# Starting the split weights of each stage 16 bytes further into longer tiles, in a one-core decoder block

## The chip, the cores and the metric

The kernel runs on one core of one Trainium2 chip. The metric is the device time in microseconds, as the median of three runs of the same kernel. Its work goes over five engines that run side by side: TensorE (PE, with its weight loads shown apart as PEld), VectorE (DVE), ScalarE (ACT), GpSimd (POOL) and SyncE (SP), which issues most transfers.

## What is computed

The reference is one layer of a decoder block on x of 512 tokens by 2048 features, all in float32. It is, cut to what matters:

```python
def reference(x, ...):
    h = rmsnorm(x, attn_pre_norm)
    m = token_mixer(h, w_in, ...)          # proj = h @ w_in (6160 columns)
                                           # 4 heads of gated linear attention, 4 of differential attention
                                           # concatenated, then @ w_o (2048 x 2048)
    x = x + rmsnorm(m, attn_post_norm)
    h = rmsnorm(x, ffn_pre_norm)
    f = conv_ffn(h, w_ffn_in, conv_w, conv_b, w_ffn_out)
    return x + rmsnorm(f, ffn_post_norm)

def conv_ffn(h, w_ffn_in, conv_w, conv_b, w_ffn_out):
    up = h @ w_ffn_in                      # 2048 x 11264
    a, b = up[..., :D_FF], up[..., D_FF:]  # D_FF = 5632
    a = causal depthwise convolution of a, width 3
    return (gelu(a) * b) @ w_ffn_out       # 5632 x 2048
```

## The kernel before

**Products in three parts.** TensorE multiplies in a reduced float32 format, so every operand is held as a high and a low part: `hi` is the value rounded to that format and `lo` the remainder. A product is the sum of three matmuls, hi·hi, hi·lo and lo·hi, into one bank of PSUM. The activations stand for a whole stage in the tiles `ah` and `al`. The weights come from HBM in granules of 128 partitions by 1024 values: `load` brings one into a tile `raw` (four buffers), and `granule` (L106) makes its two parts, `whi` on ACT (L114) and `wlo` on DVE (L115). Both have three buffers of 4096 bytes in each partition, so the split can run at most two granules ahead of the matmuls that read it. All of these buffers, and each slice of them that a matmul reads, begin at a multiple of 256 bytes within the partition. Where `granule` is given a `spare` pool, the parts go to the tiles `xhi` and `xlo` instead.

**Two kinds of matmul.** In `mm_t` (L150 to L152) and in the products of the first feed-forward matrix, `up_prods` (L897 to L899), the weights are the stationary operand, 128 by 128, and the activations stream past, 512 or 256 columns of them. In `mm_n` (L168 to L170), `down_prods` (L994 to L996) and the last part (L1101 to L1103) the activations are stationary and 512 columns of the weights stream.

**Stages in order of time.** `first_half` norms and transposes x and starts the first projection. The mixer follows: `proj_n` and `proj_t` compute the projections of w_in, and between their granules the function `step` lets small pieces of the attention heads run (the list `fill`). Then comes the output projection (three columns by `proj_n`, the fourth written out by hand in `to_ffn`), which ends in the first matmuls of the feed-forward part. The rest of that part uses a seven-product scheme for 2x2 blocks: 20 units `ups` of the first matrix, two for each of ten groups, then 10 units `downs` of the second. A unit has seven segments (x0, z0, y0, z1, x1, y1, y2) of two granules. After every second up unit, `token_sums` writes the products of this group to DRAM: three of the blocks as they are and four sums, s5, s2, s7 and s3 in this order, each added on DVE into a tile of 256 KB with the tag `sum` (L965) and put out by a transfer on SP. The down units read them back.

**What sets the order.** In three places the order on PE, ACT, DVE and POOL is the program's own (`manual_schedule`). Elsewhere a scheduler orders the instructions ahead of time, from its own estimate of when each can start; on the chip each engine then works through its list in order. When a pool of tiles is closed and another takes its place (`fa.close()`, then the pool `ff`), the first writers of the new pool wait until all work on the old one is done, its transfers to DRAM among them.

**Other pools that the change touches.** `small` holds columns of statistics (eight buffers of each), the tag `tmp` of the pool `mx` holds the working tiles of the attention heads (six buffers), and the tag `sum` those of `token_sums` (four buffers).

Of the kernel before, what the change touches and what calls it, by code (L numbers as in the profile page):

```python
# [9 lines left out]
F32 = mybir.dt.float32  # L10
F32R = mybir.dt.float32r
# [6 lines left out]
P = 128  # L18
D = 2048
S = 512  # L20
# [3 lines left out]
GH, GDK, GDV, RANK = 4, 128, 256, 16  # L24
# [6 lines left out]
GR = 1024  # L31
# [4 lines left out]
def hybrid_layer(ctx: ExitStack, tc: tile.TileContext, x, attn_pre_norm, w_in, w_alpha_up, b_alpha,  # L36
# [10 lines left out]
    def dma(o, i):  # L47
        return nc.sync.dma_start(out=o, in_=i)
# [7 lines left out]
    mm = nc.tensor.matmul  # L56

    const = ctx.enter_context(tc.tile_pool(name="const", bufs=1))
    small = ctx.enter_context(tc.tile_pool(name="small", bufs=8, side="right"))
    few = ctx.enter_context(tc.tile_pool(name="few", bufs=1, side="right"))  # L60
    psm = ctx.enter_context(tc.tile_pool(name="psm", bufs=4, space=PSUM))
    psa = ctx.enter_context(tc.tile_pool(name="psa", bufs=4, space=PSUM))
# [12 lines left out]
    wpool = ctx.enter_context(tc.tile_pool(name="w", bufs=3))  # L75

    def bank(pool=None):
        return (pool or psa).tile([P, 512], F32, name="bank", tag="bank")
# [5 lines left out]
    def step(n=None):  # L84
        pace[1] += pace[0]
        while pace[1] >= 1.0:
            pace[1] -= 1.0
            while fill:
                try:
                    next(fill[0])  # L90
                    break
                except StopIteration:
                    fill.pop(0)
# [6 lines left out]
    def load(src, a):  # L100
        raw = wpool.tile([P, GR], F32, name="raw", tag="raw", bufs=4)
        dma(raw.rearrange("p (a b) -> p a b", a=a), src)
        return raw

    def granule(src, a, raw=None, spare=None, bufs=4):
        if raw is None:  # L106
            raw = load(src, a)
        if spare:
            hi = spare.tile([P, GR], F32R, name="xhi", tag="xhi", bufs=bufs)
            lo = spare.tile([P, GR], F32R, name="xlo", tag="xlo", bufs=bufs)  # L110
        else:
            hi = wpool.tile([P, GR], F32R, name="whi", tag="whi")
            lo = wpool.tile([P, GR], F32R, name="wlo", tag="wlo")
        act(hi, raw, AF.Copy)  # L114
        tt(lo, raw, hi.bitcast(F32), ALU.subtract)  # L115
        r = "p (a b) -> p a b"
        return hi.rearrange(r, a=a), lo.rearrange(r, a=a)
# [24 lines left out]
    def mm_t(banks, g, w, t0, t1):  # L142
        for n in range(2):
            for k in range(4):
# [6 lines left out]
                mm(o, wh, al[:, t0:t1, kk, :], start=False, stop=False)  # L151
                mm(o, wl, ah[:, t0:t1, kk, :], start=False, stop=sp)  # L152


    def proj_t(w3, col, emit):
        banks = [bank(psm) for _ in range(2)]
        for g in range(KT // 4):
            mm_t(banks, g, granule(w3[:, 4 * g:4 * g + 4, col:col + 256], 4), 0, NT)
            if g == KT // 4 - 1:
                for n in range(2):  # L160
                    emit(n, banks[n])
            step()
# [8 lines left out]


    def proj_n(w3, col, emit, order=tuple(range(KT)), first=0, banks=None):
        if banks is None:
            banks = [bank(psm) for _ in range(NT)]
        for g in range(first, KT // 2):
            w = granule(w3[:, order[2 * g]:order[2 * g] + 2, col:col + 512], 2)
            for t in range(NT):
                mm_n(banks, t, g, w)
                if g == KT // 2 - 1:  # L180
                    emit(t, banks[t])
            step()
# [3 lines left out]
    mx = mixer.enter_context(tc.tile_pool(name="mx", bufs=6))  # L186

    def big8(name):
        return mx.tile([P, 2048], F32, name=name, tag="big8", bufs=6)
# [2 lines left out]
        return mx.tile([P, S], F32, name=name, tag="qk", bufs=6)  # L192

    def tmp(name, shape=(P, S)):
        return mx.tile(list(shape), F32, name=name, tag="tmp")


    def first_half(c):
# [150 lines left out]

    def forget_gate():  # L350
        gar = tmp("gar").rearrange("p (k r) -> p k r", r=RANK)[:, :KT, :]
        dma(gar, w_in3[:, :, C_GA:C_GA + RANK])
        gas = mx.tile([P, KT, 80], F32R, name="gas", tag="big8", bufs=6)
        nc.vector.memset(gas.bitcast(F32), 0.0)
        split(gas[:, :, 0:RANK], gas[:, :, 64:64 + RANK], gar)
        wup = mx.tile([80, GH * GDK], F32, name="wup", tag="tmp")
        nc.vector.memset(wup, 0.0)
        dma(wup[0:RANK, :], w_alpha_up[0])
        dma(wup[64:64 + RANK, :], w_alpha_up[0])
        yield  # L360
        gab = bank()
        gav = gab[:80, :].rearrange("p (t c) -> p t c", c=P)
        for k in range(KT):
            mm(gav, gas[:, k, :], ah[:, :, k, :], start=k == 0, stop=False)
            mm(gav, gas[:, k, :], al[:, :, k, :], start=False, stop=k == KT - 1)
        gaT = mx.tile([80, S], F32, name="gaT", tag="tmp")
        nc.vector.tensor_copy(gaT, gab[:80, :])
        yield

        a = big8("za")  # L370
        for h in range(GH):
            zb = bank()
            mm(zb, wup[:, h * P:(h + 1) * P], gaT, start=True, stop=True)
            bcol = cols[:, h:h + 1]
            act(a[:, h * S:(h + 1) * S], zb, AF.Abs, bias=bcol)
            ts(bcum[h], zb, bcol, 0.0, ALU.add, ALU.min)
            if h % 2:
                yield
# [241 lines left out]
    def to_ffn():  # L620
# [91 lines left out]
        mm_t(bb2, 3, wb[3], 2, 4)  # L712
        return ba, list(zip(bb, bb2))

    with tc.manual_schedule(engines=IN_ORDER):
        ba, bb = to_ffn()
    wo.close()
# [13 lines left out]
    fp = fa.enter_context(tc.tile_pool(name="fa", bufs=2))  # L731
# [223 lines left out]
    def token_sums(gi, u0, u1):  # L955
        c, i = (gi - 1) // 2, (gi - 1) % 2
        T = [slice(0, 256), slice(256, 512)]
        a11, a21, a12, a22 = u0[:, :, T[0]], u0[:, :, T[1]], u1[:, :, T[0]], u1[:, :, T[1]]

        def put(n, src):  # L960
            dma(sd[c][n][:, i, :].rearrange("p (n t) -> p n t", n=2), src)

        def add(n, x, y, op):
            t = fp.tile([P, 2, 256], F32, name=n, tag="sum", bufs=4)
            tt(t, x, y, op)  # L965
            put(n, t)
            return t

        put("a11", a11)
        put("a12", a12)  # L970
        put("a22", a22)
        s5 = add("s5", a21, a22, ALU.subtract)
        s2 = add("s2", s5, a11, ALU.subtract)
        add("s7", a11, a21, ALU.subtract)
        add("s3", s2, a12, ALU.add)
# [50 lines left out]
    for i, u in enumerate(ups):  # L1026
        nxt = ups[i + 1] if i + 1 < len(ups) else None
        if i == 0:
            u.x0()
            u.z0()  # L1030
        u.y0()
        u.z1()
        if i == 0:
            for h, r in enumerate(s7raw):
                split(up["s7"][0][:, h], up["s7"][1][:, h], r)
        if nxt is None:
            prepare(0, "a11", flat_tile())
        u.x1()
        if nxt is None:
            prepare(0, "s5", flat_tile())  # L1040
        u.y1()
        if nxt is not None:
            nxt.x0()
            u.y2()
            nxt.z0()
        else:
            downs = [down_unit(c, cb) for c in range(NG // 2) for cb in range(2)]
            prepare(0, "s2", flat_tile())
            downs[0].x0()
            prepare(0, "s3", flat_tile())  # L1050
            u.y2()
# [8 lines left out]
    for i, u in enumerate(downs):  # L1060
        nxt = downs[i + 1] if i + 1 < len(downs) else None
        nc_ = (i + 1) // 2
        first = i % 2 == 0
        last_cb = i % 2 == 1 and nxt is not None

        if first and i:
            prepare(i // 2, "s3")
        u.y0()
        if first:
            prepare(i // 2, "a12")  # L1070
        u.z1()
        if first:
            prepare(i // 2, "s7")
        u.x1()
        if first:
            prepare(i // 2, "a22")
        if last_cb:
            prepare(nc_, "a11")
        u.y1()
        if last_cb:  # L1080
            prepare(nc_, "s5")
        if nxt is not None:
            nxt.x0()
        if last_cb:
            prepare(nc_, "s2")
        u.y2()
        if nxt is not None:
            nxt.z0()


    def ffn_out_weights(gi, c):
# [65 lines left out]
    for q, at in enumerate(((3, 1), (0, 0))):  # L1157
        raw = ff.tile([P, GR], F32, name="st", tag="st", bufs=4)
        dma(raw, ud0[:, 2 * q:2 * q + 2, :].rearrange("p n t -> p (n t)"))
        hi, lo = (piece(v, *at) for v in (ah, al))  # L1160
# [34 lines left out]
```

## Time and profile before

| | |
|---|---|
| three runs | 2189.55, 2192.62 and 2193.9 us, median 2192.62 |
| the profiled execution's own time | 2189.8 us |
| its span, first to last instruction | 2188.1 us |
| PE busy | 2152.7 us (98%), 13009 matmuls |
| DVE busy | 1418.9 us (65%) |
| ACT busy | 901.2 us (41%) |
| POOL busy | 204.6 us (9%) |
| mean granted TensorE clock | 0.996 |

All times of an event are counted from the first instruction. Busy time of PE counts overlapping matmuls once, so a PE at 100% only says that there was always a matmul under way. The pace of the matmuls is better read from how many of them fall into a window of time. In the tables of groups each row has a line of the kernel, an engine, an operation, the tiles written and read, the count, the busy time and the mean duration in ns of one, and then the time that the engine stood idle just before it. A row of waits names who waited, for whom, the total in us, how often, and the longest.

### The profile page before, as it was taken

What the parts mean: (1) busy time and instruction counts of PE and PEld (TensorE: products, weight loads), DVE (VectorE), ACT (ScalarE), POOL (GpSimd) and SP (SyncE); (2) the same over time, 40 slices, a digit from 0 to 9 for tenths busy, and PEclk for the clock granted to TensorE, in tenths of its full rate; (3) what the DMA queues carried; (4) which work ended last, traced back from release to release, by engine and by line L of the source; (5) the groups of instructions that cost most, each with busy time, mean ns of one, the idle gap of its engine ahead of it and who ended that gap; (6) DMA issues with size and microseconds to landing.
All of it is one profiled execution on the core that took longest, in us unless ns stands there. A gap on an engine that the chain in (4) does not pass through costs nothing.

```text
span 2188.1 us, 31879 instructions
## 1 busy us (share of the span) xinstructions
PE 2152.7 (98%) x13009; PEld 1921.7 (88%) x13009; DVE 1418.9 (65%) x1722; ACT 901.2 (41%) x1162; POOL 204.6 (9%) x245
## 2 busy tenths in 40 slices
PE   7999999999999999999999999999999999999997
PEld 6878888888888889899999999999999878787886
DVE  5345554444453245886786776776777777888987
ACT  4233332333342233453443444444444464544433
POOL 1000000000000000011111111011011011011101
PEclk9999999999999999999999999999999999999999
DMA  6322222223224344447657667567567678677663
GB/s 210 103 68 79 76 78 77 78 77 87 78 87 166 104 154 154 124 109 179 154 126 183 145 136 181 138 150 175 134 157 178 173 212 218 173 187 184 151 175 136
DMA packets 218471, 303.83 MB, mean 139 GB/s; under 512 B 11776, under 2 KB 155572, under 8 KB 216404
## 3 DMA queue, kind: packets, MB, share of 16 engines
q1 hardware_dynamic: 165204, 238.87, 32.4%
q0 software_dynamic: 53120, 62.92, 18.5%
q8 instruction: 102, 1.67, 0.3%
q14 instruction: 45, 0.37, 0.0%
HBM read 273.97 MB, written 27.79 MB: 138 GB/s over the span
## 4 chain that ended last, share of the span: by engine, by line
issue 50%; PE 42%; POOL 4%; DVE 2%; DMA 1%; ACT 1%; POOLq 0%; SPq 0%; DVEq 0%; ACTq 0%
PE bank L168 7%; PE bank L169 7%; PE bank L170 7%; PE bank L152 5%; PE bank L150 5%; PE bank L151 4%; POOL rt L846 2%; POOL raw L846 2%; PE bank L417 1%; PE bank L995 1%; PE bank L996 1%; PE bank L994 1%; PE bank L485 1%; PE bank L516 1%; PE bank L135 1%
## 5 line engine op out<-in xcount | busy, mean ns | idle before, releaser
L115 DVE TENSOR_TENSOR wlo<-raw,whi 128x1024 fp32r<-128x1024 f32 x307 | 374.7, 1223 | 357.8 <-ACT whi L114 346.7
L114 ACT ACTIVATE whi<-raw 128x1024 fp32r<-128x1024 f32 x307 | 324.6, 1058 | 604.7 <-PE bank L898 185.6
L899 PE MATMUL bank<-ah,wlo 128*128 128x256 f32 x1280 | 362.9, 284 | 0.0
L898 PE MATMUL bank<-al,whi 128*128 128x256 f32 x1280 | 362.9, 284 | 0.0
L897 PE MATMUL bank<-ah,whi 128*128 128x256 f32 x1280 | 362.9, 284 | 0.0
L115 DVE TENSOR_TENSOR wlo<-rt,whi 128x1024 fp32r<-128x1024 f32 x220 | 268.1, 1222 | 114.9 <-ACT whi L114 114.6
L114 ACT ACTIVATE whi<-rt 128x1024 fp32r<-128x1024 f32 x220 | 232.1, 1058 | 260.9 <-PE bank L898 201.3
L897 PEld LDWEIGHTS bank<-ah,whi 128*128 128x128 f32 x1280 | 246.3, 192 | 0.1
L898 PEld LDWEIGHTS bank<-al,whi 128*128 128x128 f32 x1280 | 246.2, 192 | 0.1
L899 PEld LDWEIGHTS bank<-ah,wlo 128*128 128x128 f32 x1280 | 246.2, 192 | 0.0
L168 PE MATMUL bank<-whi,ah 128*128 128x512 f32 x600 | 237.5, 399 | 0.8 <-ACT ah L127 0.8
L169 PE MATMUL bank<-wlo,ah 128*128 128x512 f32 x600 | 236.3, 394 | 0.0
L170 PE MATMUL bank<-whi,al 128*128 128x512 f32 x600 | 235.5, 394 | 0.0
L150 PE MATMUL bank<-ah,whi 128*128 128x512 f32 (+1 forms) x512 | 196.4, 384 | 0.0
L152 PE MATMUL bank<-ah,wlo 128*128 128x512 f32 (+1 forms) x512 | 194.9, 381 | 0.0
L151 PE MATMUL bank<-al,whi 128*128 128x512 f32 (+1 forms) x512 | 194.8, 380 | 0.0
L995 PE MATMUL bank<-wlo,ah 128*128 128x512 f32 x420 | 164.1, 391 | 2.2 <-DVE wlo L115 2.2
L996 PE MATMUL bank<-whi,al 128*128 128x512 f32 x420 | 163.6, 390 | 0.0
L994 PE MATMUL bank<-whi,ah 128*128 128x512 f32 x420 | 156.4, 391 | 0.6 <-DVE acc L1002 0.6
L170 PEld LDWEIGHTS bank<-whi,al 128*128 128x128 f32 x600 | 113.4, 189 | 24.3 <-DVE al L128 0.3
L168 PEld LDWEIGHTS bank<-whi,ah 128*128 128x128 f32 x600 | 113.4, 189 | 24.1 <-ACT ah L127 1.2
L169 PEld LDWEIGHTS bank<-wlo,ah 128*128 128x128 f32 x600 | 113.5, 189 | 23.6 <-DVE wlo L115 0.5
(251 smaller groups left out, 4110.9 us busy)
## 6 DMA issues: line engine op xcount, KB each, us to landing
raw<-in_w_in_dram SPq DMA_DIRECT2D x96, 512.0 KB, 3.7
raw<-in_w_ffn_in_dram SPq DMA_DIRECT2D x96, 512.0 KB, 4.7
raw<-in_w_ffn_out_dram SPq DMA_DIRECT2D x48, 512.0 KB, 6.3
rt<-in_w_ffn_in_dram SPq DMA_DIRECT2D x40, 512.0 KB, 5.6
rt<-in_w_ffn_in_dram POOLq DMA_DIRECT2D x40, 512.0 KB, 5.9
raw<-in_w_ffn_in_dram POOLq DMA_DIRECT2D x40, 512.0 KB, 7.0
raw<-in_w_o_dram SPq DMA_DIRECT2D x32, 512.0 KB, 3.7
rt<-in_w_ffn_out_dram SPq DMA_DIRECT2D x20, 512.0 KB, 6.9
```

Source lines behind the costliest of these rows:

```text
L114: act(hi, raw, AF.Copy)
L115: tt(lo, raw, hi.bitcast(F32), ALU.subtract)
L150: mm(o, wh, ah[:, t0:t1, kk, :], start=st, stop=False)
L151: mm(o, wh, al[:, t0:t1, kk, :], start=False, stop=False)
L152: mm(o, wl, ah[:, t0:t1, kk, :], start=False, stop=sp)
L168: mm(banks[t], ah[:, t, s, :], w[0][:, k, :], start=st, stop=False)
L169: mm(banks[t], ah[:, t, s, :], w[1][:, k, :], start=False, stop=False)
L170: mm(banks[t], al[:, t, s, :], w[0][:, k, :], start=False, stop=sp)
L897: mm(o, wh, sh[:, :, kk, :], start=start and kk == 0 and n == 0, stop=False, **NOW)
L898: mm(o, wh, sl[:, :, kk, :], start=False, stop=False, **NOW)
L899: mm(o, wl, sh[:, :, kk, :], start=False, stop=kk == HK - 1, **NOW)
L995: mm(b[j], sh[:, o:o + P], w[1][:, q, :], start=False, stop=False, **NOW)
```

## The change

The tiles `whi` and `wlo` become 128 values (512 bytes) longer in each partition, 4608 bytes instead of 4096, and the granule lies in them from `4 * shift[0]` values on, that is 16 bytes times a number that is set stage by stage: 0 to 11 for the twelve projections by `proj_t` in the mixer, 1, 3, 5, 7, 9, 11, 2, 4 and 6 for the first nine by `proj_n`, 0 for the part written out in `to_ffn` and for the second pair of the feed-forward part, 0 to 19 for the up units, 16 to 25 for the down units and 0 for the end. `xhi` and `xlo` stay as they were. Six tiles that are 512 bytes longer take 3072 bytes of each partition; three other tags give up buffers: `small` goes from eight buffers to four, `tmp` from six to five, and `sum` from four to three. All pools behind the weights begin 3072 bytes further on. No instruction is added or removed.

The order of the instructions on SP and POOL stays the same. On PE it differs at some thirty-five places in the stage of the linear-attention heads (about 160 to 380 us), by a few products each, and at one more at about 1750 us, where one product of a down segment now stands ahead of ten others; on ACT and DVE it differs in the same stage of the heads.

```diff
-    small = ctx.enter_context(tc.tile_pool(name="small", bufs=8, side="right"))
+    small = ctx.enter_context(tc.tile_pool(name="small", bufs=4, side="right"))
...
+    shift = [0]
+    SHIFT = 128
+
     def granule(src, a, raw=None, spare=None, bufs=4):
...
         else:
-            hi = wpool.tile([P, GR], F32R, name="whi", tag="whi")
-            lo = wpool.tile([P, GR], F32R, name="wlo", tag="wlo")
+            sl = slice(4 * shift[0], 4 * shift[0] + GR)
+            hi = wpool.tile([P, GR + SHIFT], F32R, name="whi", tag="whi")[:, sl]
+            lo = wpool.tile([P, GR + SHIFT], F32R, name="wlo", tag="wlo")[:, sl]
...
+    tshift = list(range(12))
+    nshift = [1, 3, 5, 7, 9, 11, 2, 4, 6]
...
     def proj_t(w3, col, emit):
+        shift[0] = tshift.pop(0) if tshift else 0
...
     def proj_n(w3, col, emit, order=tuple(range(KT)), first=0, banks=None):
+        shift[0] = nshift.pop(0) if nshift else 0
...
     def tmp(name, shape=(P, S)):
-        return mx.tile(list(shape), F32, name=name, tag="tmp")
+        return mx.tile(list(shape), F32, name=name, tag="tmp", bufs=5)
...
+    shift[0] = 0
     with tc.manual_schedule(engines=IN_ORDER):
         ba, bb = to_ffn()
...
-            t = fp.tile([P, 2, 256], F32, name=n, tag="sum", bufs=4)
+            t = fp.tile([P, 2, 256], F32, name=n, tag="sum", bufs=3)
...
     for i, u in enumerate(ups):
...
+        shift[0] = i
         u.y0()
...
     for i, u in enumerate(downs):
...
+        shift[0] = 16 + i
         u.y0()
...
+    shift[0] = 0
+
 
     def ffn_out_weights(gi, c):
```

More of the change, by code (lines that the diff above doesn't have):

```diff
@@ L355, in forget_gate @@
         split(gas[:, :, 0:RANK], gas[:, :, 64:64 + RANK], gar)
-        wup = mx.tile([80, GH * GDK], F32, name="wup", tag="tmp")
+        wup = mx.tile([80, GH * GDK], F32, name="wup", tag="tmp", bufs=5)
         nc.vector.memset(wup, 0.0)
@@ L365, in forget_gate @@
             mm(gav, gas[:, k, :], al[:, :, k, :], start=False, stop=k == KT - 1)
-        gaT = mx.tile([80, S], F32, name="gaT", tag="tmp")
+        gaT = mx.tile([80, S], F32, name="gaT", tag="tmp", bufs=5)
         nc.vector.tensor_copy(gaT, gab[:80, :])
```

## The prediction

> **What bounds the kernel now.** I read the totals of the page first, then the windows, to see how many matmuls fall into a stretch of time, then PE's waits, then the order of time around the largest of them. The totals:
>
> ```profile
> span 2188.1 us, 31879 instructions
> PE 2152.7 (98%) x13009; PEld 1921.7 (88%) x13009; DVE 1418.9 (65%) x1722; ACT 901.2 (41%) x1162; POOL 204.6 (9%) x245
> ```
>
> PE always has a matmul under way, but that does not say what a matmul costs. The windows do. Their columns are the stretch, its length, busy time and count of each engine, the granted clock, and the transfers:
>
> ```profile
> 150.00:620.00 470.00, 469.53 (x2229) 390.05 (x2228) 237.68 (x461) 163.50 (x310) 29.68 (x64) 1.00 0.26 78
> 700.00:800.00 100.00, 100.00 (x443) 82.88 (x442) 32.24 (x32) 28.83 (x40) 0.00 (x0) 1.00 0.30 101
> 960.00:1700.00 740.00, 740.00 (x6169) 740.00 (x6169) 544.31 (x552) 339.66 (x371) 94.36 (x74) 1.00 0.65 155
> 1745.00:1754.00 9.00, 2.34 (x10) 1.68 (x9) 4.53 (x7) 2.03 (x3) 0.00 (x0) 0.74 0.57 204
> 1754.00:1765.00 11.00, 10.96 (x37) 8.26 (x37) 9.79 (x9) 8.94 (x12) 1.19 (x1) 0.75 0.88 285
> 1780.00:2000.00 220.00, 217.95 (x955) 178.70 (x954) 184.77 (x193) 107.78 (x113) 27.04 (x23) 1.00 0.68 181
> 1800.00:1900.00 100.00, 100.00 (x443) 82.88 (x442) 82.46 (x86) 49.80 (x52) 13.12 (x11) 1.00 0.78 207
> ```
>
> From 960 to 1700 us (up units, 256 columns) a matmul starts every 740 / 6169 = 0.120 us. At 700 to 800 us (output projection) and at 1800 to 1900 us (down units), both 512 columns, it is 100 / 443 = 0.226 us, though DVE is busy 32 us in the one and 82 us in the other. From 256 to 512 columns the pace grows by 0.106 us, so 256 columns cost 0.106 and each matmul pays some 13 ns beside its columns. It is the same at every hour and whatever the other engines do. PE's own pace bounds the kernel; its idle stretches are few:
>
> ```profile
> PE bank L135 <- DVE xt L229: 10.5, 2, 9.5
> PE bank L994 <- ACT xhi L114: 6.7, 1, 6.7
> PE bank L995 <- DVE wlo L115: 2.2, 5, 0.5
> PE bank L508 <- DVE s L501: 0.5, 1, 0.5
> ```
>
> The first is the start, which the change leaves alone. The second is the passage from the up to the down units at 1746 us, where the clock falls too: 0.74 and 0.75 in the two windows there. So a change can act in two ways: on the 13 ns or the columns of 13,000 matmuls, or on the passage.
>
> **The shifted starts, on PE.** With a shift other than zero, by the numbers in the code: as stationary operands, 1,056 matmuls in eleven of the twelve `proj_t` and 6,288 in the up units; as streaming operands, 1,632 in the `proj_n` and 1,260 in the down units (140 granules less the quarter that goes to `xhi`, times 12 matmuls). That is 7,344 + 2,892 = 10,236 of 13,009. Nothing here starts off a multiple of 64 bytes on PE, so the price must be bounded. The nearest row is the forget gate, whose stationary slices of 80 columns begin 320 bytes apart, every other one off the multiples of 128:
>
> ```profile
> 124.47 0.40 PE L364 MATMUL bank<-ah,gas 128*80 128x512 f32 x1
> 131.58 0.39 PE L365 MATMUL bank<-al,gas 128*80 128x512 f32 x1
> ```
>
> These are the first and the last of 32 in a row: 7.11 / 31 = 0.229 us each, against 0.226 elsewhere: at most 3 ns more, in a stretch between other work. That operands can disturb each other by some ns is seen after each interruption of PE; two stretches of one granule, soon after its start and later:
>
> ```profile
> 173.83 0.40 PE L152 MATMUL bank<-ah,wlo 128*128 128x512 f32 x1
> 175.45 0.39 PE L150 MATMUL bank<-ah,whi 128*128 128x512 f32 x1
> 176.14 0.39 PE L150 MATMUL bank<-ah,whi 128*128 128x512 f32 x1
> 178.40 0.39 PE L151 MATMUL bank<-al,whi 128*128 128x512 f32 x1
> ```
>
> Seven intervals of 0.231 us, then ten of 0.226: a pace that settles within about ten matmuls, in the same buffers. Low end: each shifted matmul sheds the whole 13 ns, 10,236 x 13 ns = 133 us saved. High end: each pays them once more, 133 us lost. A stationary operand that loads more slowly has cover, because transposes, which stream only 128 columns and so run at the pace of the loads, start more often than the 0.120 us of the up units:
>
> ```profile
> 652.63 1.91 PE L135 MATMUL bank<-ident,oa 128*128 128x128 f32 x16
> ```
>
> (1.91 - 0.27 for the last one's own length) / 15 = 0.109 us, so up to 11 ns of a slower load stay hidden. I take zero, by the forget gate, which is nearest; 3 ns on each would be 31 us, and stay in the first rival.
>
> **The shifted starts, on ACT and DVE.** Every split now writes off the old multiples. On DVE the trace has an operation that starts 4 or 8 bytes off, the convolution, beside two of the same kind that start even:
>
> ```profile
> L746 DVE SCALAR_TENSOR_TENSOR u<-u,cols 128x510 f32<-128x510 f32 x40 | 29.8, 745 | 0.0
> L745 DVE SCALAR_TENSOR_TENSOR u<-u,cols 128x511 f32<-128x511 f32 x40 | 29.0, 745 | 0.0
> L651 DVE SCALAR_TENSOR_TENSOR xr<-m,rs,g 128x512 f32<-128x512 f32 x16 | 10.9, 747 | 4.8 <-POOL rs L123 4.8
> L115 DVE TENSOR_TENSOR wlo<-raw,whi 128x1024 fp32r<-128x1024 f32 x307 | 374.7, 1223 | 357.8 <-ACT whi L114 346.7
> L114 ACT ACTIVATE whi<-raw 128x1024 fp32r<-128x1024 f32 x307 | 324.6, 1058 | 604.7 <-PE bank L898 185.6 <-PE bank L170 158.0 <-PE bank L151 100.6
> ```
>
> 745 against 747 ns: no price there, so I take zero. ACT shows no such pair; if its 1.058 us grew by a tenth, the 605 us that it idles before these splits cover it. The narrowest cover is DVE's in the down units: 220 - 184.8 = 35 us free over 220 / 2.72 = 81 granules (12 matmuls of 0.226 us each), 0.43 us a granule. A split on DVE would have to slow from 1.22 to 1.65 us before PE waited.
>
> **Three `sum` buffers for four sums.** s3 now takes the buffer of s5 and must wait until s5's transfer has landed. DVE stands in that wait, and behind it the next splits. In the first nine groups the four are spread out. The first of them, on DVE and SP, and the time to landing of the first group pair (smallest, median, largest):
>
> ```profile
> 1020.13 0.69 DVE L965 TENSOR_TENSOR s<-u 128x512 f32<-128x512 f32 x1
> 1025.94 0.69 DVE L965 TENSOR_TENSOR s<-s,u 128x512 f32<-128x512 f32 x1
> 1020.85 6.13 SPq L48 DMA_DIRECT2D sd0s<-s  x4
> DMA to landing us min/median/max: 2.0/2.4/5.4
> ```
>
> s5's transfer is issued at 1020.85 and lands about 1023.3, s3 starts at 1025.94: 2.6 us to spare. With the longest landing, 5.4 us, DVE would wait 0.3 us, and it has 740 - 544 = 196 us free in this stage; the splits are two granules ahead, 2 x 24 x 0.120 = 5.8 us. Nothing. In the tenth group nothing stands between the four, and the first writers of the next pool wait behind the last transfer:
>
> ```profile
> 1746.43 0.69 DVE L965 TENSOR_TENSOR s<-u 128x512 f32<-128x512 f32 x1
> 1748.36 0.68 DVE L965 TENSOR_TENSOR s<-s,u 128x512 f32<-128x512 f32 x1
> 1747.14 2.25 SPq L48 DMA_DIRECT2D sd4s<-s  x4
> sd4s<-s SPq DMA_DIRECT2D x4, 256.0 KB, 2.1
> 1751.42 1.09 ACT L1000 ACTIVATE accp<-bank 128x512 f32<-128x512 f32 x2 [8.44 <-DMA sd4s<-s]
> 1753.50 1.22 PE L994 MATMUL bank<-xhi,ah 128*128 128x512 f32 x2 [6.66 <-ACT xhi L114]
> 1755.78 0.63 PE L994 MATMUL bank<-xhi,ah 128*128 128x512 f32 x1
> 1756.21 0.63 PE L995 MATMUL bank<-xlo,ah 128*128 128x512 f32 x1
> ```
>
> s5 is issued at 1747.14 and lands 2.1 us later, at 1749.24; s3 started at 1748.36 and will start at 1749.24, 0.9 us later. Its transfer, accp, `xhi` and PE follow by the same: **+0.9 us**, on the path. PE then runs at half pace (0.43 us, the last two rows), for (9 x 0.26 + 11 x 0.25) x 2 = 10.2 us of lowered clock, of which some 6 lie after the restart. If the clock comes back at the same instant, the later start shortens the slow stretch by 0.9 us and gives back 0.45; if it comes back later, each us more at half clock costs 0.5. I take 0. [...]
>
> **Six to five `tmp`, eight to four `small`.** In the linear-attention heads the second working tile of a level must now wait for the matmuls of the level but one before it; the lists of PE, ACT and DVE are reordered there. POOL, which computes the statistics, waits for the others, and not they for it, with this as the longest such row:
>
> ```profile
> POOL ms L121 <- ACT jk L459: 221.0, 14, 123.2
> ```
>
> So `small` is taken at zero; without that cover it would cost about a wait of L508's size, 0.5 us. For `tmp`, PE waited 0.5 us in 470 (L508, above). A head piece that comes too early for its tiles stalls PE, and all behind it, by about such a wait; bounds 0 and, with four heads and two such pieces in each, 8 x 0.5 = 4 us. I take **+0.5 us**. Nothing excludes a small gain, since the new order may also miss the one wait of 0.5 us. The swap at 1750 us moves one matmul (0.226 us) ahead of the 6.7 us wait: below nothing by 0.2, not counted. SP's and POOL's lists do not move.
>
> **The sum.** 0 (shifts) + 0.9 (passage) + 0.5 (heads) = +1.4 us. The profiled execution takes 2189.8 us (span 2188.1 and 1.7 around it) and would take 2191.2. The median of the runs, 2192.62, stands 2.8 us above it, so the forecast is **2194.0 us**, by itself between 2190 and 2198. 0.2%, 4.4 us, is about what a measurement of this kernel can tell from no change; so this is no change.
>
> **The rivals.**
> *Off starts cost the streaming read (24%).* A streaming operand that begins off a larger unit needs one read more in each matmul. For it: no row shows such a start, the 3 and 5 ns above, and that a ns or two counts when paid thousands of times. Against it: the pace that settles. At half of the 13 ns, 2,892 x 6.5 ns = 19 us: 2213 us, slower by 0.9%. It decides from 4.4 us / 2,892 = 1.5 ns on.
> *The shorter rings stall the heads (13%).* [...] For it: the new lists rest on estimates of times. Against it: PE waited 0.5 us there.
> *The 13 ns are a collision (11%).* Weights and activations all begin at multiples of 256 bytes, so a load and a stream may collide at each change of operand, and unequal starts part them. At half of the 13 ns on 10,236 matmuls: -67 us, 2127 us, faster. It decides from 4.4 / 10,236 = 0.43 ns on. Against it: the 13 ns are the same for all three weight buffers, for loads and streams that start at different times, and in the forget gate. [...]
>
> **How the numbers follow.** The forecast has 52%: 46 within 0.2%, 3 on each side beyond. The first two rivals are slower, 24 + 13; the third is faster, 11. That makes 14% faster, 46% the same, 40% slower. The range, 2188 to 2215, holds the forecast but for its lower edge (51), the rings (13) and the first rival up to a little beyond its price (16), 80 in all.
>
> **What would show it.** Windows of the changed kernel: x6169 in 740 us of the up units if shifts are free, and 443 in 100 us of the output projection and of the down units; the first rival shows fewer in the last two alone, and more with odd shifts than with even ones if the unit is 32 bytes; the third shows more in all. L114 and L115 at 1058 and 1223 ns. The tenth group's s3 about 0.9 us later after its s5, and PE's wait at L994 7.6 us instead of 6.7. PE's waits between 150 and 620 us at 0 to 4 us. The forecast fails most easily on the pace: one ns more in every shifted matmul is 10 us.

## The result, and the profile after

The changed kernel takes 2196.56 us (median, 2195.59 to 2202.34) and the kernel before 2192.19 us beside it: a ratio of 1.0023, 95% interval 1.0015 to 1.0031. It is slower by 0.23%. The forecast was 2194.0 us, the range 2188 to 2215. The number came close by luck: two large effects of opposite sign almost cancel, and the prediction had put both at nothing.

The profiled execution took 2195.74 us. Its totals:

```profile
span 2194.0 us, 31894 instructions
PE 2157.8 (98%) x13009; PEld 1909.4 (87%) x13009; DVE 1417.2 (65%) x1722; ACT 903.0 (41%) x1162; POOL 203.9 (9%) x245
```

The 15 instructions more than before are all waits on semaphores.

The windows of the changed kernel, with the same columns as those of before:

```profile
150.00:620.00 470.00, 469.49 (x2199) 384.60 (x2198) 233.15 (x456) 161.09 (x304) 28.94 (x64) 1.00 0.26 77
700.00:800.00 100.00, 100.00 (x434) 81.15 (x433) 29.53 (x30) 27.02 (x42) 0.00 (x0) 1.00 0.30 95
960.00:1690.00 730.00, 730.00 (x6169) 730.00 (x6168) 539.43 (x546) 337.39 (x366) 93.67 (x73) 1.00 0.66 157
960.00:1700.00 740.00, 740.00 (x6254) 740.00 (x6253) 547.63 (x556) 344.70 (x375) 94.95 (x74) 1.00 0.67 158
1780.00:2000.00 220.00, 219.80 (x953) 178.49 (x952) 183.78 (x191) 109.77 (x114) 26.23 (x22) 1.00 0.68 181
1800.00:1900.00 100.00, 100.00 (x433) 80.97 (x432) 83.50 (x88) 50.85 (x54) 14.31 (x12) 1.00 0.74 194
```

The kernel before, in the first 730 us of its up units:

```profile
960.00:1690.00 730.00, 730.00 (x6085) 730.00 (x6085) 535.53 (x543) 333.93 (x364) 94.36 (x74) 1.00 0.65 154
```

With 512 columns a matmul now takes 100 / 434 = 0.230 us in the output projection and 100 / 433 = 0.231 us in the down units, 4 to 5 ns more than the 0.226 us of before (443 in both). With 256 columns it takes 740 / 6254 = 0.1183 us, 1.7 ns less than 0.120 us. The granted clock is 1.00 in all of these rows, as before, so a slower clock is not the reason.

How far the changed kernel lags behind the kernel before, by the start of the n-th matmul in both traces, tells what each stage adds:

| at (us of the kernel before) | 150 | 300 | 620 | 820 | 960 | 1200 | 1500 | 1725 | 1780 | 1900 | 2150 |
|---|---|---|---|---|---|---|---|---|---|---|---|
| changed kernel, lag in us | 0.7 | 2.6 | 7.5 | 12.0 | 12.1 | 7.3 | 4.1 | 1.4 | 2.9 | 5.2 | 5.9 |

The projections lose 12 us, the up units gain 10.7 us, the passage and the down units lose 4.5 us. Behind the passage the lag is known to some 2 us only: between 1900 and 2005 us PE waits 1.9 us, for splits above all, in the trace of before and 0.2 us in the other (the lag falls from 5.2 to 3.5 us there), and the trace of run 3 below, with the paces of before, ends 1.7 us ahead of it.

PE's waits in the changed kernel (lines of `granule` are 5 further on, those of the down units 11):

```profile
PE bank L140 <- DVE xt L239: 10.7, 2, 9.8
PE bank L1005 <- ACT xhi L119: 8.4, 2, 7.4
PE bank L1006 <- DVE wlo L120: 1.8, 4, 0.8
PE bank L518 <- DVE s L511: 0.5, 1, 0.5
```

The heads still wait 0.5 us (L518), and the passage waits 7.4 us where it waited 6.7; the other 1.0 us of its row (L1005) is a wait that is new. In the order of time around the passage, s3 (the fourth sum) waits for the transfer of s5, as the prediction had it; the last number in brackets is the idle time before the instruction:

```profile
1748.18 0.69 DVE L976 TENSOR_TENSOR s<-u 128x512 f32<-128x512 f32 x1
1748.90 3.12 SPq L48 DMA_DIRECT2D sd4s<-s  x4
...
1750.97 0.69 DVE L976 TENSOR_TENSOR s<-s,u 128x512 f32<-128x512 f32 x1 [0.78 <-DMA sd4s<-s]
1753.92 1.08 ACT L1011 ACTIVATE accp<-bank 128x512 f32<-128x512 f32 x2 [9.18 <-DMA sd4s<-s]
...
1756.00 1.22 PE L1005 MATMUL bank<-xhi,ah 128*128 128x512 f32 x2 [7.39 <-ACT xhi L119]
...
1777.95 1.06 ACT L119 ACTIVATE xhi<-raw 128x1024 fp32r<-128x1024 f32 x1 [6.98 <-DMA raw<-in_w_ffn_out_dram]
1779.06 0.73 PE L1005 MATMUL bank<-xhi,ah 128*128 128x512 f32 x2 [1.03 <-ACT xhi L119]
```

The windows of the passage, with the granted clock:

```profile
1745.00:1754.00 9.00, 3.18 (x13) 1.98 (x11) 5.86 (x7) 0.08 (x1) 0.00 (x0) 0.97 0.38 146
1754.00:1765.00 11.00, 8.96 (x30) 6.80 (x31) 7.80 (x7) 8.39 (x11) 1.19 (x1) 0.71 0.80 292
```

The clock is lowered for (9 x 0.03 + 11 x 0.29) x 2 = 6.9 us here and was for 10.2 us before; behind PE's restart that leaves 4.3 us at half clock (granted 0.50 from 1755 to 1760 us, most matmuls 0.43 us apart) instead of 6.1 (0.43 us as well). So the lag, which grows from 1.7 to 2.5 us in the wait, is back at 1.7 us at 1768 us: the shorter slow stretch gave the longer wait back. The 2.9 us at 1780 us come from the second wait, of 1.0 us, for a granule that came late from DRAM. Why it came late is not shown; run 3, which keeps the four `sum` buffers, loses 0.5 us at the same place.

The splits themselves have not slowed:

```profile
L120 DVE TENSOR_TENSOR wlo<-raw,whi 128x1024 fp32r<-128x1024 f32 x307 | 374.8, 1223 | 391.1 <-ACT whi L119 387.6 <-PE bank L909 3.1
L119 ACT ACTIVATE whi<-raw 128x1024 fp32r<-128x1024 f32 x307 | 325.0, 1060 | 600.5 <-PE bank L179 163.9 <-PE bank L909 149.4 <-PE bank L156 106.3
```

**The pace unit by unit.** The starts are set per unit, so the trace of the changed kernel is a sweep in itself. The mean time from one matmul to the next, within units that keep one start (in units of 16 bytes):

| start x 16 bytes | 0 | 1 | 2 | 3 | 4 | 5 | 6 | 7 | 8 | 9 | 10 | 11 | 12 | 13 | 14 | 15 | 16 |
|---|---|---|---|---|---|---|---|---|---|---|---|---|---|---|---|---|---|
| up units, 256 columns, ns | 120.0 | 118.3 | 118.3 | 117.8 | **113.3** | 118.8 | 118.7 | 120.0 | 120.0 | 118.3 | 120.0 | 118.1 | 117.8 | 116.7 | 116.7 | 120.0 | 120.0 |
| `proj_t`, 512 columns, ns | 226.7 | 226.7 | 232 to 235, starts 2 to 10 | | | | | | | | | 230.1 | | | | | |

`proj_n` shows 227 to 228 at start 0, 228.9 at 4 and 230.5 to 233.4 at the others; the down units 227.1 at 16 and 229.5 to 233.5 at 17 to 25. In the up units 16 (256 bytes) is as 0, and 17 to 19 (118.3, 118.3 and 117.8 ns) are as 1 to 3. So, as far as these starts show it, the start counts modulo 256 bytes; with 512 columns it costs up to 8 ns, and nothing in the one `proj_t` that begins at 16 bytes; with 256 columns it gives up to 7 ns. The unit at start 4 stands out; three windows of the changed kernel, within the units at 3, 4 and 5:

```profile
1075.00:1105.00 30.00, 30.00 (x258) 30.00 (x257) 18.95 (x18) 11.89 (x13) 5.16 (x4) 1.00 0.84 194
1113.00:1143.00 30.00, 30.00 (x267) 30.00 (x267) 22.22 (x24) 15.12 (x17) 5.13 (x4) 1.00 0.87 207
1153.00:1183.00 30.00, 30.00 (x255) 30.00 (x254) 18.98 (x18) 11.59 (x12) 5.13 (x4) 1.00 0.83 194
```

The middle one holds 267 matmuls where those beside it hold 258 and 255, with DVE, ACT and the transfers busier, not quieter.

### The profile page after: what moved, and what is told of

Read it like the earlier page. It is cut to its first block, busy times and chain, and to the rows that moved or that the text cites. A ratio compares the mean times of both kernels' runs of the same rounds, so it can differ in the third digit from the quotient of the medians.

```text
span 2194.0 us, 31894 instructions
## 1 busy us (share of the span) xinstructions
PE 2157.8 (98%) x13009; PEld 1909.4 (87%) x13009; DVE 1417.2 (65%) x1722; ACT 903.0 (41%) x1162; POOL 203.9 (9%) x245
## 4 chain that ended last, share of the span: by engine, by line
PE 49%; issue 43%; POOL 3%; DVE 2%; DMA 1%; ACT 1%; POOLq 0%; SPq 0%; DVEq 0%; ACTq 0%
PE bank L178 6%; PE bank L179 6%; PE bank L177 6%; PE bank L157 5%; PE bank L155 5%; PE bank L156 5%; POOL rt L857 2%; PE bank L909 2%; PE bank L908 2%; PE bank L910 2%; POOL raw L857 1%; PE bank L427 1%; PE bank L1006 1%; PE bank L1007 1%; PE bank L1005 1%
## 5 line engine op out<-in xcount | busy, mean ns | idle before, releaser
L120 DVE TENSOR_TENSOR wlo<-raw,whi 128x1024 fp32r<-128x1024 f32 x307 | 374.8, 1223 | 391.1 <-ACT whi L119 387.6
L119 ACT ACTIVATE whi<-raw 128x1024 fp32r<-128x1024 f32 x307 | 325.0, 1060 | 600.5 <-PE bank L179 163.9
L910 PE MATMUL bank<-ah,wlo 128*128 128x256 f32 x1280 | 359.1, 281 | 0.0
L119 ACT ACTIVATE whi<-rt 128x1024 fp32r<-128x1024 f32 x220 | 232.4, 1060 | 251.9 <-PE bank L909 191.9
L908 PEld LDWEIGHTS bank<-ah,whi 128*128 128x128 f32 x1280 | 241.5, 189 | 0.1
L910 PEld LDWEIGHTS bank<-ah,wlo 128*128 128x128 f32 x1280 | 241.5, 189 | 0.0
L909 PEld LDWEIGHTS bank<-al,whi 128*128 128x128 f32 x1280 | 241.3, 189 | 0.1
L1005 PE MATMUL bank<-whi,ah 128*128 128x512 f32 x420 | 157.5, 393 | 0.0
```

The costliest lines, as they stand in the source:

```text
L908: mm(o, wh, sh[:, :, kk, :], start=start and kk == 0 and n == 0, stop=False, **NOW)
L909: mm(o, wh, sl[:, :, kk, :], start=False, stop=False, **NOW)
L910: mm(o, wl, sh[:, :, kk, :], start=False, stop=kk == HK - 1, **NOW)
```

## The experiments

Each ratio is against the kernel before on the same chip.

**1. The shorter rings alone.** The changed kernel, all starts at zero:

```diff
-            sl = slice(4 * shift[0], 4 * shift[0] + GR)
+            sl = slice(0, GR)
```

> The changed kernel with all starts put back to zero; the longer tiles, the fewer buffers and the order of the instructions stay. If the starts alone moved the pace of the matmuls: windows again at 0.120 us a matmul in the up units and 0.226 in the output projection and the down units, and the time at before + 0.9 (passage) + 0.5 (heads), about 2193.5 us, ratio 1.0006. If the fewer buffers and the new order made the loss of 4.4 us: about 2196.5 us, ratio 1.002, with PE waits in the heads.

Measured: 2190.79 us against 2189.06 us, ratio 1.0006 (0.9997 to 1.0016). Windows of this run:

```profile
700.00:800.00 100.00, 100.00 (x443) 82.81 (x442) 31.81 (x31) 28.59 (x40) 0.00 (x0) 1.00 0.30 101
960.00:1690.00 730.00, 730.00 (x6086) 730.00 (x6085) 534.80 (x543) 333.02 (x362) 94.70 (x74) 1.00 0.65 154
```

Both paces of before are back (443; 730 / 6086 = 0.1199 us). This trace lags the one of before by 0.3 us at 620 us, 1.0 at 820, 2.4 at 1780 and 1.4 at the end. The medians are 1.7 us apart, and the interval reaches from 0.7 us faster to 3.5 us slower, so the 1.4 us that were forecast for the rings fit but can't be told from nothing. The changed paces come from the starts alone.

**2. The up units at zero.** The changed kernel with the up units put back to zero; its other stages keep their starts:

```diff
-        shift[0] = i
+        shift[0] = 0
         u.y0()
```

> The changed kernel with only the up units put back to zero: the shifted projections and down units alone. If the parts add up by their windows: + 12 us in the projections, + 5 to 7 in the down units, + 1.4 of the buffers, and no gain in the up units: about 2207 us, ratio 1.009. If the forecast's zero price held and the loss came from elsewhere: about 2196 us again.

Measured: 2206.14 us against 2190.23 us, ratio 1.0074 (1.0057 to 1.0091).

```profile
700.00:800.00 100.00, 100.00 (x434) 81.13 (x433) 29.76 (x30) 26.71 (x42) 0.00 (x0) 1.00 0.27 95
960.00:1690.00 730.00, 730.00 (x6086) 730.00 (x6085) 535.00 (x543) 333.16 (x362) 92.39 (x72) 1.00 0.65 154
```

The lag is 11.7 us at 820 us, still 11.7 at 1725 us, 11.6 at 1800 us and 15.7 at 2150 us. With run 1 the parts can be told apart. Off starts cost the projections 11.7 - 1.0 = 10.7 us and the down units (15.7 - 11.6) - (1.4 - 2.4) = 5.1 us; in the changed kernel they gave the up units 10.7 us back. With the 1.4 us of run 1 the two losses make 17.2 us, 1.5 more than this trace shows, because the passage added 1.4 us in run 1 (1.0 to 2.4) and nothing here. By the medians this run loses 15.9 us; less the 10.7 us of the up units that is 5.2, where the changed kernel lost 4.4. So the parts add up to within 1.5 us.

**3. Weights and activations moved together.** The kernel before with a tile in front of all the others 64 bytes longer, so that weights and activations, and all other tiles behind it, begin 64 bytes further on and keep their distances:

```diff
-    small = ctx.enter_context(tc.tile_pool(name="small", bufs=8, side="right"))
+    small = ctx.enter_context(tc.tile_pool(name="small", bufs=7, side="right"))
...
-    pad = const.tile([P, 32], F32, name="pad")
+    pad = const.tile([P, 48], F32, name="pad")
```

> The kernel before, with a tile ahead of all others 64 bytes longer, so that activations and weights all begin 64 bytes further on and keep their distances (small has seven buffers instead of eight, for the room). If the distance between the weights and the activations counts: paces as before, 0.120 and 0.226 us, about 2192 us. If the start of a tile itself counts: 0.1134 us in the up units (44 us less) and 0.229 to 0.233 in the stages with 512 columns (about 4,900 x 4 ns = 20 us more), about 2168 us.

Measured: one execution, 2188.16 us (before: 2187.23 to 2192.21). Its windows:

```profile
700.00:800.00 100.00, 100.00 (x443) 82.84 (x442) 32.23 (x32) 28.86 (x40) 0.00 (x0) 1.00 0.29 101
960.00:1690.00 730.00, 730.00 (x6085) 730.00 (x6085) 535.24 (x543) 333.90 (x363) 94.58 (x74) 1.00 0.65 154
```

Neither pace moves. A shift of 64 bytes changes the pace when the weights alone have it (run 4) and not when the activations have it too: what counts is where the weights begin relative to the activations. This was tried for 64 bytes only.

**4. All up units at 64 bytes.** From run 1, the start of the fast unit in all twenty up units, zero elsewhere:

```diff
+            at = 4 * shift[0] if up else 0
+            sl = slice(at, at + GR)
...
+    shift[0] = 4
     for i, u in enumerate(ups):
...
-        shift[0] = i
```

> The changed kernel with the starts at zero everywhere but in the up units, where all 20 begin 64 bytes in. If the pace depends on the start within 256 bytes, as the unit with that shift showed (0.1134 us a matmul against 0.120): 6,720 x 6.6 ns = 44 us less in the up units, the other stages as before, + 1.4 us of the buffers: about 2149 us, ratio 0.980. If that unit was fast for another reason (its place, its neighbours): the mean over the shifted units, 0.1183 us, 6,720 x 1.7 ns = 11 us less, about 2182 us, ratio 0.995.

Measured: 2173.79 us against 2189.06 us, ratio 0.9936 (0.9921 to 0.9951).

```profile
700.00:800.00 100.00, 100.00 (x443) 82.70 (x441) 32.66 (x31) 28.37 (x40) 0.00 (x0) 1.00 0.30 103
960.00:1690.00 730.00, 730.00 (x6200) 730.00 (x6200) 548.02 (x558) 341.74 (x373) 93.77 (x73) 1.00 0.66 157
```

The same stretch of 30 us, at the same start, as that of the unit at 4 above, here with 257 matmuls instead of 267:

```profile
1153.00:1183.00 30.00, 30.00 (x257) 30.00 (x256) 23.40 (x25) 12.66 (x13) 4.25 (x4) 1.00 0.55 145
```

It is faster than both kernels, but at 730 / 6200 = 0.1177 us, not 0.1133, and 2173.79 us lies between the two times expected. Throughout this stage the intervals of single matmuls lie at 117 to 119 ns, where the unit at 64 bytes in the changed kernel repeated 114, 113, 113. Only the last matmuls of the stage, after an interruption at about 1722 us, fall into 113. So one start can hold more than one steady pace. That what ran before decides which is a guess at this point.

**5. The same with a run-up.** Run 4 with the first unit and the first two segments of the second at 48 bytes, then 64 bytes, as the unit at 4 of the changed kernel followed the one at 3:

```diff
-    shift[0] = 4
+    shift[0] = 3
     for i, u in enumerate(ups):
...
+        if i == 1:
+            shift[0] = 4
```

> The run with 64 bytes in the up units, but its first unit (and the first two segments of the second) begins 48 bytes in; from there on 64 bytes. If the pace at a start has more than one steady form and which one depends on what ran before (0.1178 us after the stage of 512 columns, 0.1134 after a unit at 48 bytes): the later 18 units at 0.1134 us, 6,288 x 6.6 + 432 x 2.2 ns = 42 us less than at zero, about 2149 us, 25 us faster than the run with 64 bytes alone. If the form depends on the start alone, and something else slowed that run: 0.1178 us again, about 2174 us.

Measured: 2173.57 us, ratio 0.9918 (0.9896 to 0.994); the four executions took 2176.36, 2165.09, 2174.34 and 2172.81 us. The profiled one holds x6200 in the 730 us again. The run-up did not bring the fast pace there. But it was not the run-up of the changed kernel either: its unit at 48 bytes ran at 118.3 ns, and the one ahead of the fast unit at 117.8 ns. So 48 bytes has more than one pace as well, and what decides between the paces of one start stays open. The execution of 2165 us may have held the fast one for a part of the stage; no trace shows it.

**6. Load and stream at another step.** In the up units the high and low values of a granule alternate in one tile of the kernel before, so that a weight load steps 8 bytes a column instead of 4:

```diff
+            both = wpool.tile([P, 2 * GR], F32R, name="w", tag="w")
+            if mix:
+                pair = both.rearrange("p (x two) -> p x two", two=2)
+                hi, lo = pair[:, :, 0], pair[:, :, 1]
```

> The kernel before with the two parts of a granule in one tile; in the up units their values alternate (hi, lo, hi, lo), so a weight load steps 8 bytes a value instead of 4, at no shift. A load takes 0.109 us for 128 values (0.85 ns each), the stream 0.106 us for 256 (0.41 ns each), so a load with 8 byte steps goes through the memory as fast as the stream. If the 13 ns are load and stream meeting in the same part of the memory while one overtakes the other: they stop meeting, 0.109 to 0.113 us a matmul, 6,720 x 7 to 11 ns = 47 to 74 us less, 2118 to 2145 us. If only the start counts: 0.120 us, about 2192 us. If a stepped load is slower in itself: over 0.120 us and slower than before.

Measured: 2192.86 us against 2189.06 us, ratio 1.0016 (1.0006 to 1.0025), and x6081 in the same 730 us, 0.120 us each. The pace did not move. The load time that the expectation went by, 0.109 us, was an estimate from the interval between the transposes of the kernel before. My picture, that a load costs something where it overtakes the stream at the same place modulo 256 bytes, is not confirmed. ACT is busy for longer here (355.6 us in that window against 333.0 in run 1). The loss of 3.8 us lies outside the pace: by this trace, the slowest of the ten executions, the up units lose 0.5 us between 960 and 1700 us, and the rest comes before and behind them.

**7. A sweep of other starts, the two parts set apart.** The changed kernel, with the start of `whi` and of `wlo` given singly, in values of 4 bytes:

```diff
-    shift = [0]
+    shift = [(0, 0)]
...
+            sh, sl = (slice(v, v + GR) for v in shift[0])
...
+    ushift = same(0, 1, 2, 3, 14, 15, 17, 18) + [(16, 0), (0, 16), (16, 32), (32, 16), (16, 48), (48, 16), (32, 0), (0, 32),
+                                                 (16, 8), (16, 12), (16, 20), (16, 24)]
```

> The changed kernel with other starts, given for the high and the low part apart, in values of 4 bytes: in the projections by proj_t 48, 52, 56, 60, 1, 2, 3, 64 for both, then (16,0), (0,16), (32,0), (0,32); by proj_n 32, 40, 48, 52, 56, 60, 1, 2, then (0,16); in the up units 0, 1, 2, 3, 14, 15, 17, 18, then (16,0), (0,16), (16,32), (32,16), (16,48), (48,16), (32,0), (0,32), (16,8), (16,12), (16,20), (16,24); in the down units 40, 44, 48, 52, 56, 60, 1, 2, then (0,16), (16,0). If whole lines of 16 bytes count and not the bytes in them: 1, 2 and 3 values at the pace of zero (0.120 and 0.2267 us), 64 values (256 bytes) too. If every start but zero costs a stage of 512 columns something: all of these between 0.2267 and 0.235 us, none below. If each part counts by itself: the mixed starts lie between the paces of their two parts.

Measured: one execution, 2195.05 us (before: 2188.71 to 2192.71). The up units by the values at which `whi` and `wlo` begin; the five that are left out lie between 117.8 and 119.5 ns:

| whi, wlo (4 bytes) | 0, 0 | 1, 1 | 2, 2 | 3, 3 | 14, 14 | 16, 0 | 0, 16 | 16, 32 | 32, 16 | **16, 48** | **48, 16** | 32, 0 | 0, 32 | 16, 8 | 16, 12 |
|---|---|---|---|---|---|---|---|---|---|---|---|---|---|---|---|
| ns a matmul | 120.0 | 118.3 | 115.6 | 116.7 | 117.8 | 117.8 | 117.8 | 118.2 | 119.4 | **113.3** | **113.3** | 118.4 | 119.1 | 119.3 | 117.0 |

The unit at 16, 48 in a window of 30 us:

```profile
1432.00:1462.00 30.00, 30.00 (x267) 30.00 (x266) 22.01 (x24) 15.11 (x17) 5.13 (x4) 1.00 0.86 202
```

Four things follow. Starts of 4, 8 or 12 bytes change the pace too. Two pairs give 113.3 ns, with `whi` at 64 bytes and `wlo` at 192, or the other way. The two parts don't count each by itself: 0 and 32 values (128 bytes) each run at 120.0 ns when both parts have them, but 32, 0 and 0, 32 run at 118.4 and 119.1. And with 512 columns every new start costs something (228.9 to 237 ns against 226.7), while 64 values (256 bytes) run at 226.7 ns, as zero does.

**8 and 9. The two pairs in all up units.** Run 1, with the pair in the up units alone:

```diff
+            sh, sl = (slice(v, v + GR) for v in ((16, 48) if up else (0, 0)))
+            hi = wpool.tile([P, GR + SHIFT], F32R, name="whi", tag="whi")[:, sh]
```

> All splits begin at zero again, but in the up units whi begins 64 bytes and wlo 192 bytes into its tile. If the pace belongs to the pair of starts (theory): the unit that had this pair in the sweep ran at 0.1134 us a matmul, so 6,720 matmuls save 6.6 ns each against 0.120, 44 us, and with the 1.4 us of the rings the time is about 2148 us; 960 to 1690 us hold about 6,440 matmuls. If the 0.1134 us came from the units that ran before (rival, by the run with all units at 64 bytes): the stage stays at another steady pace, 0.1178 as in that run, and the time is about 2175 us with some 6,200 matmuls in the same window.

> The same with the two starts exchanged, whi at 192 bytes and wlo at 64. Theory (the pair sets the pace): 0.1133 us as in the sweep, about 2148 us, 6,440 matmuls in 960 to 1690 us. Rival (what ran before sets it): here the sweep came to this pair from the other one, already at 0.1134, so this run would fall back to 0.1178 to 0.120 us, 2175 to 2192 us, also where the run with 64 and 192 bytes holds 0.1134.

Measured: 64 / 192 bytes 2149.0 us (2147.0 to 2151.3) against 2189.39 us, ratio 0.9818 (0.9801 to 0.9836); 192 / 64 bytes 2154.04 us, ratio 0.9842 (0.9824 to 0.986). The first of them is 1.8% faster than the kernel before and the best version found. Its windows, then its waits at the passage (L1005) and in the up units (L910):

```profile
700.00:800.00 100.00, 100.00 (x443) 82.81 (x442) 32.35 (x31) 28.67 (x40) 0.00 (x0) 1.00 0.30 102
960.00:1690.00 730.00, 728.80 (x6407) 727.28 (x6406) 561.96 (x573) 351.77 (x386) 98.85 (x77) 1.00 0.68 163
```

```profile
PE bank L1005 <- ACT xhi L119: 8.2, 2, 7.4
PE bank L910 <- DVE wlo L120: 1.7, 4, 0.8
```

Apart from the interruptions the up units run at 113.3 to 113.4 ns in every stretch of 100 us from 1000 us on. The window holds 6,407 matmuls and not the 6,440 expected, because PE now waits for splits in the up units, which it had not done before (1.2 of the 1.7 us of L910 lie in this window), and because it has slower intervals besides: the 728.80 us in which PE is busy would hold 728.80 / 0.11334 = 6,430 at the fast pace, 23 more than they do, 2.6 us.

The run of 192 / 64 bytes, over the whole window and where it mixes two paces:

```profile
960.00:1690.00 730.00, 728.82 (x6399) 728.29 (x6398) 562.81 (x573) 351.09 (x385) 98.15 (x77) 1.00 0.68 162
1400.00:1500.00 100.00, 100.00 (x871) 99.96 (x870) 74.52 (x78) 47.22 (x52) 15.42 (x12) 1.00 0.72 170
```

It falls from 113.3 to about 119 ns for some 30 us twice, from 1416 and from 1571 us on, each time after an interruption of PE, and then returns to 113.3 by itself; after another interruption, at 1340 us, it stays at 113.3. So the rival, that the history alone sets the pace, falls for these pairs: both find the fast pace straight after the stages of 512 columns. But the theory holds only in part, since one of them shows a second pace too. What the pairs show is that they fall back into the fast pace, where a start of 64 bytes for both parts stayed at 117.8 ns.

**10. Such pairs with 512 columns.** Up units at 64 / 192 bytes, and twelve pairs in the other stages, one for each projection or down unit:

```diff
+    pairs = [(16, 48), (48, 16), (16, 32), (32, 48), (48, 32), (32, 16), (8, 40), (24, 56), (48, 0), (0, 48), (32, 56), (20, 52)]
+    tshift = list(pairs)
+    nshift = pairs[:9]
+    ushift = [(16, 48)] * 20
+    dshift = pairs[:10]
```

> The up units stay at 64 and 192 bytes. The stages of 512 columns get pairs of unequal starts for whi and wlo, another pair in each projection and each down unit: 64/192, 192/64, 64/128, 128/192, 192/128, 128/64, 32/160, 96/224, 192/0, 0/192, 128/224 and 80/208 bytes. If unequal starts 128 bytes apart shed half of the 13 ns whatever the number of columns (theory), the first two and those with 32/160, 96/224 and 80/208 show 0.220 us a matmul instead of 0.2267. If 512 columns are best with all starts at zero, as every start of the sweep before was (rival), all pairs show 0.228 to 0.236 us, and the time is about 2149 + 20 = 2169 us, one look.

Measured: one execution, 2166.41 us (before: 2190.73 us).

```profile
700.00:800.00 100.00, 100.00 (x429) 80.35 (x428) 28.71 (x30) 26.48 (x42) 0.00 (x0) 1.00 0.27 95
960.00:1690.00 730.00, 728.65 (x6421) 727.86 (x6421) 563.45 (x574) 352.03 (x387) 97.64 (x76) 1.00 0.68 162
1800.00:1900.00 100.00, 100.00 (x432) 80.75 (x432) 87.23 (x93) 45.62 (x46) 11.93 (x10) 1.00 0.64 169
```

No pair reaches 0.220 us: in undisturbed stretches of 10 us with shifted starts the mean lies between 228.9 and 234.5 ns, against 226.7 at zero. The gain of the pairs belongs to 256 columns. With 512, no start that was tried beat zero; only 16 bytes in a `proj_t` of the changed kernel, and 256 bytes, were as good.

## Why the prediction was right in its number and wrong in its main step

**"The shifted starts, on PE": "I take zero, by the forget gate, which is nearest". This step failed.** Runs 1 and 2 put in its place +10.7 us in the projections, -10.7 us in the up units and +4 to +5 in the down units. The bounds held (133 us either way), and the sum lies near zero, but because a loss and a gain happen to meet, not because the price is nothing. Two things misled. The forget gate was read as 3 ns "at most", in a short stretch between other work; that was close to the size of the effect (4 to 5 ns on average with 512 columns), and should have been carried as a price, not rounded off. Its trace says more than its mean does: its slices begin 0, 64, 128 and 192 bytes behind a multiple of 256 in turn, two matmuls to each, and the intervals repeat with these eight matmuls, 237, 227, 230, 229, 231, 227, 227 and 225 ns. The intervals went with the start there already. And one row of 512 columns was taken for 256 columns as well, where the sign is the other.

**"Off starts cost the streaming read" (first rival).** Right on the sign and nearly on the size for 512 columns: 4 to 5 ns on each, where it took 6.5 and would have decided from 1.5 on. Wrong on the reason, a further read of the streaming operand: `proj_t`, whose weights are stationary, pays as well, 3 to 8 ns at all starts but zero and 16 bytes, and there 64 and 128 bytes (233.4 and 233.2 ns) are dearer than 16 (226.7). Moving weights and activations together by 64 bytes left both paces as they were (run 3: 443 and 6085 matmuls in the two windows, as before).

**"The 13 ns are a collision" (third rival).** The up units bear out its direction, and runs 8 and 9 its size: 120.0 - 113.34 = 6.66 ns is half of the 13 ns, as this rival took it. What it did not see is that most starts give only 0 to 3 ns, and that with 512 columns other starts make it worse. That the cause is a collision is not shown (run 6, 0.120 us). The argument against it, that the 13 ns are the same for all buffers, at all times and in the forget gate, was no argument: the buffers all began at multiples of 256 bytes, and in the forget gate, the only case that differs, they are not the same (above). The relative start of the two operands alone moves the pace between 113.3 and 120.0 ns; whether their two reads are what meets is open.

**"Three sum buffers": +0.9 us at the passage.** Right about the wait: s3 starts 2.79 us after its s5 where it started 1.93 us after it, and accp, `xhi` and PE follow; PE's longest wait grew from 6.7 to 7.4 us, where the prediction had 7.6. Wrong about the time: the prediction took nothing for the clock, and the clock gave some 0.8 us back (a lag of 2.5 us behind the wait, 1.7 at 1768 us). The loss at the passage is another wait, of 1.0 us behind it.

**"Six to five tmp, eight to four small": +0.5 us.** The wait at L518 is the 0.5 us of before and no other came in the heads; run 1 lags by 0.3 us at the end of this stage. So the 0.5 us are not shown. That the trace of run 1 ends 1.4 us behind, the sum forecast for the rings, is chance: its parts are others, and it can't be told from nothing. **"The shorter rings stall the heads"** did not come about.

**"Shifted starts on ACT and DVE": zero.** Right: 1223 ns as before, and 1060 ns against 1058.

**What would show it.** The view named ahead, matmuls in a fixed window, was the right one: 434 and 433 instead of 443, and 6254 instead of 6169, tell both errors at once. The busy share (98%) and the total time tell neither.

## What to carry to other kernels

Where a stream of loads and matmuls has PE busy throughout, count matmuls in a window stage by stage before judging an edit, since two stages can move in opposite directions and leave the total still (here 10.7 us lost in the projections and 10.7 gained in the up units). How far the weights begin from the activations, modulo 256 bytes, is a parameter worth a sweep for each shape of matmul: 1.8% of this kernel lay in it for 256 columns, and with 512 nothing beat zero. A pace seen in one unit of a sweep must be tried by itself over a whole stage, because the same starts can settle at more than one pace (64 bytes for both parts: 113.3 ns in one unit, 117.7 over the stage). And where a short stretch differs from the rest by a few ns, look at its single intervals before the mean is rounded off.

## What the runs showed of the hardware that was not expected

- The pace of alternating loads and matmuls depends on the relative start of the two operands, and starts 256 bytes apart gave the same (at 256 columns 16 steps of 16 bytes 120.0 ns, as 0, and 17 steps 118.3, as 1; at 512 columns 226.7 ns at 0 and at 256 bytes): 113.3 to 120.0 ns at 256 columns, 226.7 to 237 ns at 512.
- Differences within 16 bytes count too: 0, 4, 8 and 12 bytes gave 120.0, 118.3, 115.6 and 116.7 ns. Nor are starts that differ by whole multiples of 16 bytes alike: the up units at 1, 4 and 7 times 16 bytes ran at 118.3, 113.3 and 120.0 ns.
- Intervals settle into patterns that repeat (114, 113, 113 ns, or 117 to 119 ns), and at a start of 64 bytes for both parts either holds over whole units (the changed kernel's unit at 4, and run 4). After an interruption the pace can change to the other (run 4 at 1722 us, run 9 at 1416 and 1571 us) or not (run 9 at 1340 us).
- Why this is so is not shown. That the relative start of weights and activations moves the pace is shown (the sweep and runs 1, 3, 4, 8 and 9); that two reads get in each other's way would fit it, but the one run that changed how they pass each other (run 6) left the pace where it was.
